# Attention units: projection products redealt over the units, a second output buffer, one group's evacuation and the output-projection groups placed earlier, row sums in another PSUM bank

## The chip, the cores and the metric

The kernel runs on one core of one Trainium2 chip. The metric is device time in microseconds (us), lower is better. Before the change the median of three runs was 2871.65 us (2866.72 to 2871.75). All times of the profile are from one further execution, taken with the hardware profiler; its own time is in the table below.

## The reference

Two trunk layers of a latent generator with a context prefix: layer 0 mixes tokens with differential attention, layer 1 with a state-space layer, and each is followed by an MLP. There are 1024 latent and 256 context tokens, 1024 channels, 8 heads with two 64-wide halves each. The change touches only the attention of layer 0:

```python
q_l = apply_rope(heads_qk(q_l), cos, sin) * scale
k_l = apply_rope(heads_qk(k_l), cos, sin)
...
def attend(q, k, v):
    s = jnp.einsum('bqhcd,bkhcd->bhcqk', q, k).astype(jnp.float32)
    p = jax.nn.softmax(s, axis=-1)
    w = p[:, :, 0] - lam * p[:, :, 1]
    o = jnp.einsum('bhqk,bkhe->bqhe', w.astype(v.dtype), v)
    return rmsnorm(o, subln_g) * (1.0 - lambda_init)
...
y_lat = jnp.einsum('bte,ed->btd', o_l, w_o)
```

Context queries see context keys only; latent queries see all 1280 keys. Everything is held to float32 accuracy: the kernel splits each operand into a high and a low half and makes three matmuls of each product (lines L132, L133 and L134 of the helper `mm3`: high by high, high by low, low by high).

## The kernel before

**Stages.** The attention stage runs from 219 to 895 us of the span. Ahead of it lie the norms, the value projection and head 0's queries and keys; behind it the rest of the output projection, the MLP of layer 0, and layer 1.

**Units.** The stage is a loop over 72 units, nine a head: n = 9h + u, with h from 0 to 7 and u from 0 to 8. Unit 0 of a head holds both tiles of 128 context queries; units 1 to 8 hold one tile of 128 latent queries each, against 1280 keys. Five more turns of the loop (n = 72 to 76) finish what is left. One turn does, for its own unit:

- scores on PE, 18 matmuls (L579) into PSUM banks 0 to 5 in three pieces of six; the third piece writes banks 2 and 3 beside their other contents
- two maxima on DVE (L592, 128x1280 each, which also copy the scores to SBUF), two exponentials on ACT (L602)
- on DVE the combination of the two softmaxes (`combine`, L610 to L613)

and for the unit before it:

- the transposes of the combined weights on PE (L625), in three parts: w0 (4 tiles), w1 (2) and w2 (4). w0 and w1 are as a rule split straight from PSUM, the high half by ACT (L631), the low half by DVE (L632); this is `direct`. w2 is copied out by ACT (L638) and split on POOL; this is `copied`.

Two units of queries make a pair. For a finished pair, PE multiplies the weights by the values into bank 6 (`values`), ACT copies the result to an output buffer (`pair_out`, L732), POOL squares it (L733) and a DMA stores it. A unit later PE sums the squares over each row (`pair_sums`, L739, 128x1 matmuls against ones) into bank 6, and ACT reads the sums (L740). In unit 5 of the next head, PE transposes the row factors (`norm_rows`, L758) into bank 6; five later turns multiply them in (`norm_pair`, L772 on DVE).

**Fills.** While DVE and ACT work on a unit, PE works on the projections of the next head. Those of queries and keys are six groups of eight products (three matmuls each), with 512 or 256 tokens a group, placed in units 0, 1, 2, 3, 5 and 7 (the table `AHEAD`). Each group accumulates in bank 7. `FILLS` says how its eight products are dealt over the three gaps of a unit: `(0, 1, 5, 8)` puts product 0 in the first gap, 1 to 4 in the second, 5 to 7 in the third; units not in the table have `(0, 0, 5, 8)`. Units 4, 6 and 8 have no group and another layout (`inside`). A 512-token group is emptied by `evac` (L528, L529), and then rotated, added and split by `sine`, `add` and `store` in the posts of later gaps (`next_post`; `store` is the split of ACT's L137 and DVE's L138). The two groups of context tokens (256 wide; keys in unit 1, queries in unit 2) have no rotation: their only step is `direct` (L523 on ACT, L524 on DVE). Unit 3's first product writes the bank that unit 2's group is emptied from.

**Head 7** has no next head to project. From n = 64 on it takes the output projection's groups for the first six heads instead (`wo_group`: six products of 512 columns, 18 matmuls, out by L855), one a turn, and head 7's own norm (`norm7`, L808 to L814; L812 is a 128x256 product into bank 6). Their weights are loaded and split in the same turns (`wsplit6`, its low half by POOL's L138, 128x1024).

**What sets the order.** The loop is under a manual schedule: PE, DVE, ACT and POOL execute in the order of the code. An instruction waits for the last conflicting access to the PSUM bank that it touches, even when it touches another part of the bank. In the stages behind, the framework's scheduler orders the engines by itself.

Of the kernel before, what the change touches and what calls it, by code (L numbers as in the profile page):

```python
# [13 lines left out]
KB = 256  # L14
# [56 lines left out]
class Prog:  # L71
# [578 lines left out]

    WO_BANKS = {8: 0, 9: 1, 0: 2, 1: 3, 2: 4, 3: 5, 4: 7}
    AHEAD = {0: (1, 0), 1: (1, 2), 2: (0, 2), 3: (1, 1), 5: (0, 0), 7: (0, 1)}
    FILLS = {0: (0, 1, 5, 8), 1: (0, 0, 0, 8), 2: (0, 2, 8, 8)}

    def b_start(self):

# [25 lines left out]
    def phase_b(self):  # L682
# [1 line left out]
        p0 = Ring([self.view(self.F1, 5 * i, (1280,)) for i in range(2)])  # L684
        p1 = self.view(self.F1, 10, (1280,))
        self.wraw = Ring([self.view(self.F1, 15 + 2 * i, (512,)) for i in range(3)])
        o = self.fv(6, 256)
        sq = self.adat
        self.raw = Ring([self.wv(0, 1024)])
        self.wr = Ring([(self.rv(4 * i, 4, 128), self.rv(4 * i + 2, 4, 128)) for i in range(4)])  # L690
# [37 lines left out]
        hst = self.fv(7, 3, 8, 10)  # L728

        def pair_out(h, pair):  # L730
            d = o7[pair % 2] if h == 7 else o
            nc.scalar.activation(d, pb[:, 0:256], AF.Copy)  # L732
            nc.gpsimd.tensor_tensor(sq, d, d, ALU.mult)  # L733
            if h < 7:
                self.dma(self.od[h, :, 256 * pair : 256 * pair + 256], d)

        def pair_sums(h, pair):
            for i in range(2):
                mm(pb[:, i : i + 1], sq[:, 128 * i : 128 * i + 128], self.ones, start=True, stop=True)  # L739
            nc.scalar.activation(hst[:, 1, h, 2 * pair : 2 * pair + 2], pb[:, 0:2], AF.Copy)  # L740


        def norm_calc(h, q0=0, q1=10):
# [11 lines left out]
        nloaded = []  # L755

        def norm_rows(h):
            nc.tensor.transpose(pb[0:10, 384:512], hst[:, 2, h], self.ident)  # L758
            rT = self.view(self.F1, 25, (128,))[0:10]
            nc.scalar.activation(rT, pb[0:10, 384:512], AF.Copy)  # L760
            self.dma(self.rsd[h], rT)

        def norm_load(h, pair):
# [93 lines left out]

            return [product(k) for k in range(6)], [out]

        wo_order = [8, 9] + list(range(8))  # L860

        self.qb = Ring([self.bank(7)])
        load_first()
# [12 lines left out]
        with self.manual():  # L876
            for n in range(72 + 5):
# [10 lines left out]
                if front:  # L888
# [10 lines left out]
                        qsplit = self.proj_weights(h + 2 if n else 1, 0)  # L899
                    if u == 5 and h < 6:  # L900
                        ksplit = self.proj_weights(h + 2, 1)
                if 64 <= n < 74:
                    groups = [wo_group(wo_order[n - 64])]
                fills = [[], [], []]
                if groups:
                    a = self.FILLS.get(u, (0, 0, 5, 8))
                    if n > 71:
                        a = (0, 2, 4, 6) if n == 72 else (0, 4, 6, 6)
                    fills = [groups[0][0][a[i] : a[i + 1]] for i in range(3)]
# [36 lines left out]
                if late or parts == 1:  # L946
                    if n == 73:
                        fill(0)
                    if inside:
                        values(*pv, 0, 5)  # L950
                        w0 = part(0, last)
                        values(*pv, 5)
                        w1, w2 = part(1, high), part(2, whole)
                    else:
                        if pv:
                            values(*pv)
                        w0, w1 = part(0, whole), part(1, high)
                    exps(0)
                    if inside:
                        direct(w0)  # L960
                    next_post()
                    exps(1)
                    if pv:
                        output(*pv)
                    split = norm()
                    if front:
                        self.combine(u, p, s0, sn)
                    if inside:
                        copied(w2, w1)
                    else:  # L970
                        direct(w0)
                        copied(w1)
                        if n != 73:
                            fill(0)
                        fill(1)
                        copied(part(2, whole))
                        fill(2)
                        do_sums()
                else:
                    if pv:  # L980
                        values(*pv)
                        output(*pv)
                    fill(0)
                    w0 = part(0, low)
                    if pv:
                        exps(0)
                    direct(w0)
                    next_post()
                    if not pv:
                        exps(0)  # L990
                    exps(1)
                    fill(1)
                    w2 = part(2, whole)
                    w1 = part(1, last[:, 256:512] if pv and h < 7 else self.bank(0)[:, 0:256] if n == 72 else high)
                    copied(w2)
                    if front:
                        self.combine(u, p, s0, sn)
                    direct(w1)
                    next_post()
                    fill(2)  # L1000
                    do_sums()
                    split = norm()
                if groups:
                    rest = groups[0][1]
                    rest[0]()
                    post += rest[1:]
                if split:
                    split()
# [1521 lines left out]
    def run(self):  # L2530
        tc = self.tc
        pool = lambda name, **kw: tc.tile_pool(name=name, bufs=1, **kw)
        with pool("cst") as self.cst, pool("psp", space=bass.MemoryType.PSUM) as psp, \
# [22 lines left out]
            with pool("r0") as rp, pool("fc") as cp:  # L2556
# [4 lines left out]
                    self.setup()  # L2561
                    self.phase_v()
                with pool("r1") as rp, pool("f1") as fp:
                    self.R1, self.F1 = rp.tile([128, 29 * KB], F32R, name="R1"), fp.tile([128, int(25.5 * KB)], F32, name="F1")
                    self.phase_b()
                for g in range(3):
                    for j in range(2):
# [72 lines left out]
```

## Time and profile before

| what | value |
|---|---|
| median of three runs | 2871.65 us (2866.72 to 2871.75) |
| the profiled execution, its own time | 2870.31 us |
| its span, first to last instruction | 2868.5 us |
| mean granted TensorE clock | 0.987 |
| attention stage, 219 to 895 us: busy PE / DVE / ACT / POOL | 621.1 / 525.3 / 381.2 / 370.0 of 676.0 us |
| everything behind 1000 us: busy PE / DVE | 1814.5 / 1336.8 of 1868.0 us |

How the rows are read. PE is the matmul engine, PEld its weight load, DVE the vector, ACT the scalar and POOL the GpSimd engine, SP the queue that issues DMAs. A row of windows gives a stretch of the span, its length, each engine's busy time with the number of instructions, the granted clock (1.00 is full speed), the DMA engines' mean share and GB/s. A row of waits gives the engine and line that waited, what it waited for, and total, count and longest. A row of the timeline gives start, duration, engine, line, operation, destination <- source, shape and number of instructions that run on; in brackets how long the engine was idle ahead of it, and what released it. L12 is line 12 of the kernel. PS is PSUM; H, R, F, W, FC, K, U are SBUF regions; od, Ad, Aa, wod are DRAM.

### The profile page before, as it was taken

How to read it: one execution, taken by the hardware profiler on the slowest of the kernel's cores; microseconds unless marked ns; L12 is line 12 of the kernel's file. 1: busy time of each engine (PE TensorE's matmuls, PEld its weight loads, DVE VectorE, ACT ScalarE, POOL GpSimd, SP SyncE). 2: the span in 40 equal slices, each digit the busy share in tenths (PEclk: the TensorE clock that was granted, in tenths of full speed). 3: DMA queues.
4: the chain of work that ended last, by engine and by line, in shares of the span. 5: the costliest groups of instructions: out<-in, count | busy, mean ns of one | idle time of the engine just before them, and what ended most of it. 6: DMA issues, size and time to landing. Idle time of an engine off the chain costs nothing. (4 is left out here: it accounts for less than half of the span.)

```text
span 2868.5 us, 43793 instructions
## 1 busy us (share of the span) xinstructions
PE 2721.0 (95%) x15645; PEld 2263.1 (79%) x15645; DVE 2026.8 (71%) x3024; ACT 1373.3 (48%) x2584; POOL 983.5 (34%) x822
## 2 busy tenths in 40 slices
PE   6999999999899899999999999899999999999999
PEld 4687878888677787878877778788887778888887
DVE  6357788888864477676698878799633597668566
ACT  3425555566553753333344445477443633344443
POOL 3314555565643700000020004588221243336314
PEclk9999999999999999999999999899999999999999
DMA  9953223333514448886699878479843144467544
GB/s 272 322 174 127 62 86 94 90 94 91 175 61 140 148 153 308 306 290 236 216 345 301 276 237 273 155 232 294 264 140 109 61 157 164 160 231 239 165 131 142
DMA packets 377447, 539.12 MB, mean 188 GB/s; under 512 B 38286, under 2 KB 231052, under 8 KB 374028
## 3 DMA queue, kind: packets, MB, share of 16 engines
q1 hardware_dynamic: 377228, 536.32, 57.5%
q8 instruction: 123, 2.02, 0.3%
q14 instruction: 96, 0.79, 0.1%
HBM read 367.54 MB, written 164.47 MB: 185 GB/s over the span
## 5 line engine op out<-in xcount | busy, mean ns | idle before, releaser
L132 PE MATMUL PS<-H 128*128 128x512 f32 x1072 | 420.5, 393 | 2.3 <-ACT H L137 1.5
L134 PE MATMUL PS<-H 128*128 128x512 f32 x1072 | 417.5, 390 | 3.0 <-DVE H L138 1.7
L133 PE MATMUL PS<-H 128*128 128x512 f32 x1072 | 417.7, 390 | 0.0
L132 PE MATMUL PS<-H,R 128*128 128x512 f32 (+1 forms) x828 | 307.9, 374 | 15.8 <-DVE R L524 11.6
L133 PE MATMUL PS<-H,R 128*128 128x512 f32 (+1 forms) x828 | 300.4, 363 | 0.0
L134 PE MATMUL PS<-H,R 128*128 128x512 f32 (+1 forms) x828 | 299.9, 363 | 0.0
L132 PEld LDWEIGHTS PS<-H 128*128 128x128 f32 x1072 | 201.1, 188 | 50.3 <-issue 6.2
L134 PEld LDWEIGHTS PS<-H 128*128 128x128 f32 x1072 | 201.2, 188 | 46.1 <-DVE H L138 2.6
L133 PEld LDWEIGHTS PS<-H 128*128 128x128 f32 x1072 | 201.3, 188 | 40.5
L132 PE MATMUL PS<-R,H 128*128 128x512 f32 x534 | 212.7, 399 | 3.9 <-ACT H L137 3.2
L137 ACT ACTIVATE R<-W 128x512 fp32r<-128x512 f32 (+1 forms) x185 | 129.7, 708 | 180.4 <-PE PS L133 107.6
L602 ACT ACTIVATE F<-F,stat 128x1280 f32<-128x1280 f32 x128 | 174.5, 1363 | 86.6 <-DVE F L592 86.3
L137 ACT ACTIVATE H<-U 128x640 fp32r<-128x640 f32 x216 | 131.9, 674 | 174.4 <-PE PS L133 147.3
L134 PE MATMUL PS<-R,H 128*128 128x512 f32 x534 | 210.7, 396 | 1.7 <-DVE H L138 1.7
L592 DVE TENSOR_SCALAR_CACHE_REDUCE F<-PS 128x1280 f32<-128x1280 f32 x128 | 185.4, 1485 | 34.8 <-PE PS L579 34.5
L133 PE MATMUL PS<-R,H 128*128 128x512 f32 x534 | 209.6, 393 | 0.0
L138 DVE TENSOR_TENSOR H<-U,H 128x640 fp32r<-128x640 f32 x216 | 165.6, 800 | 55.0 <-ACT H L137 54.9
L138 DVE TENSOR_TENSOR H<-W,H 128x512 fp32r<-128x512 f32 (+1 forms) x137 | 127.1, 939 | 103.2 <-ACT H L137 102.8
L132 PEld LDWEIGHTS PS<-H,R 128*128 128x128 f32 x828 | 158.6, 192 | 45.4 <-DVE R L524 13.3
L137 ACT ACTIVATE H<-W 128x512 fp32r<-128x512 f32 (+2 forms) x158 | 95.2, 613 | 189.8 <-PE PS L133 117.8
L134 PEld LDWEIGHTS PS<-H,R 128*128 128x128 f32 x828 | 158.5, 191 | 25.6 <-issue 0.8
L133 PEld LDWEIGHTS PS<-H,R 128*128 128x128 f32 x828 | 158.9, 192 | 21.1
(528 smaller groups left out, 6704.2 us busy)
## 6 DMA issues: line engine op xcount, KB each, us to landing
W<-in_mlp_w SPq DMA_DIRECT2D x176, 256.0 KB, 3.4
U<-Aa SPq DMA_DIRECT2D x108, 320.0 KB, 3.9
Aa<-FU SPq DMA_DIRECT2D x91, 320.0 KB, 4.5
Ad<-F SPq DMA_DIRECT2D x112, 256.0 KB, 2.7
W<-Ad SPq DMA_DIRECT2D x112, 256.0 KB, 2.7
FU<-in_mlp_w SPq DMA_DIRECT2D x32, 512.0 KB, 5.8
Ta<-FU SPq DMA_DIRECT2D x16, 1024.0 KB
U<-in_ada_w SPq DMA_DIRECT2D x32, 512.0 KB, 9.2
```

The source lines that it names most:

```text
L132: mm(out, ah, bh, start=first, stop=False, **kw)
L133: mm(out, ah, bl, start=False, stop=False, **kw)
L134: mm(out, al, bh, start=False, stop=last, **kw)
L137: self.nc.scalar.activation(hi, src, AF.Copy)
L138: (lo_eng or self.nc.vector).tensor_tensor(lo, src, hi.bitcast(F32), ALU.subtract)
L592: ts(p[c], self.PS[:, 1792 * c : 1792 * c + 1280], 1.0, None, ALU.mult, ALU.min, accum_out=sm[:, c : c + 1])
L602: nc.scalar.activation(p[c], p[c], AF.Exp, bias=sm[:, c : c + 1], scale=-1.0, accum_out=sn[:, 0:1] if c else s0[:, u + 1 : u + 2])
```

## The change

Six edits, all of them in the attention stage:

- `FILLS` and the default of a unit: in unit 0 products 0 to 2 stand in the first gap and 3 and 4 in the second (before: 0, and 1 to 4). In units 3, 5 and 7 product 0 moves from the second gap to the first. From n = 63 on, six-product groups are dealt 1, 3, 2 or, in turns of the other layout, 0, 4, 2 (before: 0, 5, 1 as a rule).
- `pair_out` takes one of two output buffers in turn for heads 0 to 6. The second lies at the end of `F1`, which is 1 KB larger.
- In unit 2 the context-token group is emptied right behind `direct(w1)`, ahead of `next_post` and `norm`. The call `fill(2)` stands ahead of `direct(w1)` in the code; on PE the order stays.
- `pair_sums` writes the last two columns of the first half of the score banks, `PS[:, 1790:1792]` in bank 3, except for head 7's pairs 3 and 4, which stay in bank 6.
- `norm_rows` transposes into `PS[0:10, 1280:1408]` in bank 2.
- The ten output-projection groups run in n = 63, 64, 65, 66, 68, 69, 70, 71, 72, 73 (before: 64 to 73).

```diff
-    FILLS = {0: (0, 1, 5, 8), 1: (0, 0, 0, 8), 2: (0, 2, 8, 8)}
+    FILLS = {0: (0, 3, 5, 8), 1: (0, 0, 0, 8), 2: (0, 2, 8, 8)}
...
-        o = self.fv(6, 256)
+        outs = Ring([self.fv(6, 256), self.view(self.F1, 25.5, (256,))])
...
-            d = o7[pair % 2] if h == 7 else o
+            d = o7[pair % 2] if h == 7 else outs.next()
...
         def pair_sums(h, pair):
+            b = pb[:, 0:2] if h == 7 and pair > 2 else self.PS[:, 1790:1792]
             for i in range(2):
-                mm(pb[:, i : i + 1], sq[:, 128 * i : 128 * i + 128], self.ones, start=True, stop=True)
-            nc.scalar.activation(hst[:, 1, h, 2 * pair : 2 * pair + 2], pb[:, 0:2], AF.Copy)
+                mm(b[:, i : i + 1], sq[:, 128 * i : 128 * i + 128], self.ones, start=True, stop=True)
+            nc.scalar.activation(hst[:, 1, h, 2 * pair : 2 * pair + 2], b, AF.Copy)
...
         def norm_rows(h):
-            nc.tensor.transpose(pb[0:10, 384:512], hst[:, 2, h], self.ident)
+            b = self.PS[0:10, 1280:1408]
+            nc.tensor.transpose(b, hst[:, 2, h], self.ident)
             rT = self.view(self.F1, 25, (128,))[0:10]
-            nc.scalar.activation(rT, pb[0:10, 384:512], AF.Copy)
+            nc.scalar.activation(rT, b, AF.Copy)
...
-        wo_order = [8, 9] + list(range(8))
+        wo_at = dict(zip((63, 64, 65, 66, 68, 69, 70, 71, 72, 73), [8, 9] + list(range(8))))
...
-                if 64 <= n < 74:
-                    groups = [wo_group(wo_order[n - 64])]
+                if n in wo_at:
+                    groups = [wo_group(wo_at[n])]
...
-                    a = self.FILLS.get(u, (0, 0, 5, 8))
+                    a = self.FILLS.get(u, (0, 1, 5, 8) if n < 63 else (0, 0, 4, 6) if late else (0, 1, 4, 6))
...
+                    fill(2)
                     direct(w1)
+                    now = groups and n < 63 and len(groups[0][1]) == 1
+                    if now:
+                        groups[0][1][0]()
                     next_post()
-                    fill(2)
                     do_sums()
                     split = norm()
                 if groups:
                     rest = groups[0][1]
-                    rest[0]()
+                    if late or parts == 1 or not now:
+                        rest[0]()
                     post += rest[1:]
...
-                    self.R1, self.F1 = rp.tile([128, 29 * KB], F32R, name="R1"), fp.tile([128, int(25.5 * KB)], F32, name="F1")
+                    self.R1, self.F1 = rp.tile([128, 29 * KB], F32R, name="R1"), fp.tile([128, int(26.5 * KB)], F32, name="F1")
```

The built programs show what moves. First DVE's queue in unit 2 of head 4 up to unit 3's first maxima, before. A row has line, operation, destination <- source, shape, and in brackets the engines or DMA queues that it waits for; L613 ends the combination, L632 is `direct(w1)`, L138 a store, L772 the norm of a pair, L524 the context group's evacuation, L592 the next unit's maxima:

```order
L613 SCALAR_TENSOR_TENSOR F_1851<-F_1851,stat 128x1280 [waits DVE_49]
L632 TENSOR_TENSOR R_110<-PS,R_110 128x2x128 [waits Activation_49]
L138 TENSOR_TENSOR R_1850<-FC,R_1850 128x512 [waits Activation_49]
L772 SCALAR_TENSOR_TENSOR W<-W,lamc 128x256 [waits DMAHW7_49,DMAHW0_49]
L524 SCALAR_TENSOR_TENSOR R_110<-PS,R_1850 128x256 [waits Activation_49]
L592 TENSOR_SCALAR F_1851,stat<-PS 128x1280 [waits PE_49]
```

The same piece of DVE's queue of the change (the lines behind `pair_sums` are one or two higher there):

```order
L613 SCALAR_TENSOR_TENSOR F_1851<-F_1851,stat 128x1280 [waits DVE_49]
L632 TENSOR_TENSOR R_110<-PS,R_110 128x2x128 [waits Activation_49]
L524 SCALAR_TENSOR_TENSOR R_110<-PS,R_1850 128x256 [waits Activation_49]
L138 TENSOR_TENSOR R_1850<-FC,R_1850 128x512 [waits Activation_49]
L774 SCALAR_TENSOR_TENSOR W<-W,lamc 128x256 [waits DMAHW7_49,DMAHW6_49]
L592 TENSOR_SCALAR F_1851,stat<-PS 128x1280 [waits PE_49]
```

L524 has passed the store and the norm of a pair.

Second, PE at the end of unit 1 and the start of unit 2 of a head, before: the last projection product, the row sums (L739) and the 18 score matmuls (L579; the last six are the third piece):

```order
L134 MATMUL PS<-H,R_110 128x256
L739 MATMUL PS<-lamc,adat 128x1 [waits Pool_49]
L739 MATMUL PS<-lamc,adat 128x1
L579 MATMUL PS<-R_1850 128x512 x12
L579 MATMUL PS<-R_1850 128x256 [waits DVE_49]
L579 MATMUL PS<-R_1850 128x256 x5
```

And PE at the same place in the change, where the sums are L740:

```order
L134 MATMUL PS<-H,R_110 128x256
L740 MATMUL PS<-lamc,adat 128x1 [waits DVE_49,Pool_49]
L740 MATMUL PS<-lamc,adat 128x1
L579 MATMUL PS<-R_1850 128x512 x12
L579 MATMUL PS<-R_1850 128x256
L579 MATMUL PS<-R_1850 128x256 [waits Activation_49]
L579 MATMUL PS<-R_1850 128x256 x4
```

The order of the instructions is the same; the sums wait for DVE as well (in this unit L632 of w0, which reads bank 3), and the third piece of the scores waits for ACT (the reading of the sums). In the other units the sums waited for DVE and POOL before, and wait for ACT (the copy of w2) and POOL now.

Third, PE in unit 63 (n = 63, head 7's unit 0). Before, the end of its scores (L579), ten transposes and the sums stood there, with unit 64's scores behind:

```order
L579 MATMUL PS<-R_1850 128x256 x4
L579 MATMUL PS<-R_1850,R_110 128x256 x2
L625 MATMUL PS<-ident,F_1851 128x128 x10
L739 MATMUL PS<-lamc,adat 128x1 x2
L579 MATMUL PS<-R_1850 128x512 x12
```

In the change the products of the first output-projection group (L132 to L134, 128x512) stand between and behind the transposes; the piece has the first products in the middle gap and those after the other transposes:

```order
L625 MATMUL PS<-ident,F_1851 128x128 x3
L132 MATMUL PS<-R_110,H 128x512 [waits DMAHW6_49]
L133 MATMUL PS<-R_110,H 128x512
L134 MATMUL PS<-R_110,H 128x512 [waits DMAHW7_49]
L132 MATMUL PS<-R_1850,H 128x512 [waits DMAHW0_49,Activation_49]
L133 MATMUL PS<-R_1850,H 128x512 [waits Pool_49]
L134 MATMUL PS<-R_1850,H 128x512 [waits DMAHW1_49]
L625 MATMUL PS<-ident,F_1851 128x128 x4
L625 MATMUL PS<-ident,F_1851 128x128 [waits DVE_49]
L625 MATMUL PS<-ident,F_1851 128x128
L132 MATMUL PS<-R_1850,H 128x512 [waits DMAHW0_49]
```

The second product of this piece waits for ACT and POOL, the two engines that split the group's weights; the transposes of the unit stand behind it.

## Prediction

> **What bounds the kernel now.** I read the page first, then the windows, then the waits of the attention stage, then the timeline of single units.
>
> ```profile
> span 2868.5 us, 43793 instructions
> PE 2721.0 (95%) x15645; PEld 2263.1 (79%) x15645; DVE 2026.8 (71%) x3024; ACT 1373.3 (48%) x2584; POOL 983.5 (34%) x822
> 541.00:621.00 80.00, 75.26 (x536) 64.95 (x534) 66.56 (x107) 47.43 (x95) 46.31 (x42) 0.98 0.28 85
> 780.00:895.00 115.00, 104.30 (x626) 87.30 (x627) 64.05 (x108) 48.92 (x94) 50.94 (x59) 0.94 0.23 76
> 895.00:1000.00 105.00, 93.17 (x445) 74.13 (x444) 48.72 (x54) 60.34 (x120) 58.73 (x69) 0.98 0.49 157
> 1000.00:1100.00 100.00, 100.00 (x543) 84.83 (x543) 75.44 (x116) 54.79 (x110) 5.08 (x2) 1.00 0.56 186
> ```
>
> PE is the bound: 95% of the span, and 100 of 100 us once the attention stage and the stage behind it are over (last row). So a microsecond that PE stops waiting in attention (219 to 895 us) is a microsecond of the kernel, as long as PE doesn't wait for it later. One head is the window 541 to 621: PE is idle 4.7 of 80 us, DVE busy 66.6. The idle has few names:
>
> ```profile
> PE PS L625 <- DVE F L613: 16.3, 21, 2.3
> PE PS L132 <- DVE R L524: 11.6, 7, 2.1
> PE PS L739 <- POOL R L641: 8.4, 14, 1.7
> PE PS L758 <- ACT FC L740: 2.1, 6, 0.4
> ACT FC L732 <- DMA od<-FC: 7.2, 3, 2.9
> ```
>
> Each row is total, count, longest. The transposes (L625) wait for the weights that DVE makes (L613); the first product of unit 3 (L132) waits for the direct group's evacuation (L524); the row sums (L739) and the row transpose (L758) wait for a bank. I go through these unit by unit.
>
> **Unit 3: the direct group emptied sooner, one product ahead.** Head 4, PE and then DVE:
>
> ```profile
> 558.11 2.01 PE L579 MATMUL PS<-R 64*128 64x512 f32 x18
> 560.23 0.66 PE L625 MATMUL PS<-ident,F 128*128 128x128 f32 x4
> 562.98 0.80 PE L132 MATMUL PS<-H,R 128*128 128x512 f32 x1 [2.10 <-DVE R L524]
> 566.65 0.40 PE L132 MATMUL PS<-H,R 128*128 128x512 f32 x1
> 568.03 0.82 PE L625 MATMUL PS<-ident,F 128*128 128x128 f32 x6
> 571.19 2.00 PE L579 MATMUL PS<-R 64*128 64x512 f32 x18
> 560.09 0.42 DVE L632 TENSOR_TENSOR R<-PS,R 128x256 fp32r<-128x256 f32 x1
> 560.42 0.76 DVE L138 TENSOR_TENSOR R<-FC,R 128x512 fp32r<-128x512 f32 x1
> 561.11 1.48 DVE L772 SCALAR_TENSOR_TENSOR W<-W,lamc 128x256 f32<-128x256 f32 x1
> 562.51 0.41 DVE L524 SCALAR_TENSOR_TENSOR R<-PS,R 128x256 fp32r<-128x256 f32 x1
> 565.67 0.68 DVE L632 TENSOR_TENSOR R<-PS,R 128x512 fp32r<-128x512 f32 x1
> ```
>
> From 566.65 to 568.03 PE does two products, six matmuls: 0.23 us each, 0.69 a product. The five products from 562.98 to 568.03 took 5.05 instead of 3.45: 1.6 lost at half clock. L524 stands behind L138 and L772; in the change it follows L632 at once and ends at 560.42 + 0.42 = 560.9. PE ends its scores at 560.1, so it waits 0.8 for the first product, then transposes and does four products (2.8): 564.9. The next transposes for the bank of the first (two of the six) need the L632 that ends at 566.35: DVE's own queue, which the change doesn't shorten. Then three products and the sums (0.2 + 2.1 + 0.45): the next scores at 569.2 instead of 571.2. So of 2.1 us of wait and 1.6 of half clock this head gets 2.0; without half clock the same steps give about 1.0, since L632 bounds them. Of the seven waits of the row three (heads 2 to 4) were followed by half clock: 3 x 2.0 + 4 x 1.0 = **-10.0**. What ACT and DVE had queued behind the old L524 (the store's L138, then the maxima) moves by L524's 0.4 at most.
>
> ```profile
> 480.00:490.00 10.00, 8.03 (x39) 6.30 (x36) 8.62 (x14) 5.03 (x9) 3.52 (x4) 0.83 0.14 42
> 640.00:650.00 10.00, 7.58 (x40) 5.94 (x39) 8.06 (x12) 5.12 (x11) 5.04 (x5) 1.00 0.12 40
> ```
>
> The granted clock was 0.83 in the ten microseconds of one such wait and 1.00 in another of the same length: a wait of 2 us sometimes costs a stretch of half clock (0.17 x 10 us lost is 3.4 us at half speed). The Trainium skill, "TensorE: Matmul & The Clock Gate" (Part 1), says that the clock halves after a whole idle window of about 3.4 us, the window running freely. By that rule a wait of 2 us would not do it, the dips would stay with a shorter one, and the forecast would be 2844.7 instead of the 2842.4 below. The trace decides for neither: the first row has a dip at 2 us of idle, the second has none. So I count only half of what I credit to dips, here 3 x 1.0 and in head 7 1.5: **+2.3** on the sum (0 to +4.5).
>
> **Two output buffers.** ACT's L732 waited for the store of the one buffer (last row of the waits, three times, 2.9 the longest), and in heads 2 and 3 PE waited for L732:
>
> ```profile
> 394.19 0.66 PE L625 MATMUL PS<-ident,F 128*128 128x128 f32 x4 [0.75 <-ACT FC L732]
> 475.06 0.66 PE L625 MATMUL PS<-ident,F 128*128 128x128 f32 x4 [1.06 <-ACT FC L732]
> ```
>
> Two outputs follow each other only in units 1 and 2; with a second buffer the next store to be waited for is two units old: 0.75 + 1.06 = **-1.8** (at the least 0, if DVE sets unit 3 in these heads too). SP issues as many stores of the same size as before.
>
> **Units 5, 7 and 0: products redealt.** One product more stands ahead of the transposes in 5 and 7, two more in 0.
>
> ```profile
> 590.36 1.49 DVE L592 TENSOR_SCALAR_CACHE_REDUCE F<-PS 128x1280 f32<-128x1280 f32 x1 [1.07 <-PE PS L579]
> 580.50 0.63 PE L625 MATMUL PS<-ident,F 128*128 128x128 f32 x4 [0.50 <-DVE F L613]
> 535.48 0.63 PE L625 MATMUL PS<-ident,F 128*128 128x128 f32 x4 [1.37 <-DVE F L613]
> 620.62 1.43 DVE L138 TENSOR_TENSOR R<-FC,R 128x512 fp32r<-128x512 f32 x1
> 623.38 1.49 DVE L592 TENSOR_SCALAR_CACHE_REDUCE F<-PS 128x1280 f32<-128x1280 f32 x1 [0.34 <-PE PS L579]
> 550.63 0.68 DVE L632 TENSOR_TENSOR R<-PS,R 128x512 fp32r<-128x512 f32 x1
> 550.85 0.50 PE L739 MATMUL PS<-lamc,adat 128*128 128x1 f32 x4
> ```
>
> Unit 5: 0.69 covers the 0.50, and L758, in another bank, no longer waits its 0.35; DVE is free from 589.3 and idle before unit 6's maxima (590.36, for the scores), so it is kept: 6 x 0.85 + 0.5 in head 0 = **-5.6**. In units 7, 8 and 0 the waits vanish too (0.5 + 0.3 + 1.4), but what is late next is DVE: before unit 1's maxima (623.38) it idled 0.34 us only. Its L138 took 1.43 against 0.76 in unit 3, beside a POOL instruction that starts when PE's last transposes are copied, now 1.4 us sooner: perhaps 0.6 more. So unit 1 comes 0.95 sooner. And unit 1 has a new wait: its sums now lie in the bank that L632 reads, until 551.3, where PE began them at 550.85: 0.5 lost. Behind them on PE stand unit 2's scores, and DVE waits for these. Net 0.4 a head, six heads: **-2.4** (between +3, the new wait alone, and the full 2.2 a head, -13).
>
> **Sums in free half banks.** Elsewhere they wait for ACT's copy alone instead of L632; that is the 8.4 us of L739, in units 3 and 7 counted above, in head 7 below. The next scores' third piece is now behind ACT's read of the sums; it has 1.3 us (12 of 18 matmuls of a 2.0 us block), and ACT was waiting for PE each time:
>
> ```profile
> 587.80 0.17 ACT L740 ACTIVATE FC<-PS 128x2 f32<-128x2 f32 x1 [1.28 <-PE PS L739]
> ```
>
> **Head 7: wo groups a unit sooner.**
>
> ```profile
> 772.50 1.06 PE L625 MATMUL PS<-ident,F 128*128 128x128 f32 x8 [2.27 <-DVE F L613]
> 782.25 0.98 PE L739 MATMUL PS<-lamc,adat 128*128 128x1 f32 x4 [6.14 <-DVE R L632]
> 783.16 3.57 PE L579 MATMUL PS<-R 64*128 64x512 f32 x18
> 777.04 2.34 POOL L138 TENSOR_TENSOR R<-W,R 128x1024 fp32r<-128x1024 f32 x1
> 813.04 0.58 PE L739 MATMUL PS<-lamc,adat 128*128 128x1 f32 x4 [1.56 <-POOL R L641]
> 833.59 0.58 PE L739 MATMUL PS<-lamc,adat 128*128 128x1 f32 x4 [1.67 <-POOL R L641]
> ```
>
> Unit 63 holds over 8 us of idle. A wo group (18 matmuls, 4.1 us) goes in. It doesn't run through: its fifth product needs the weights whose low half POOL finishes at 779.4, so PE still stands some 5 us, and then has 0.7, the transposes, 0.7 and the sums left: unit 64 at about 782.2, **-1.0**. Behind the waiting product stand unit 63's last transposes; POOL and ACT get them late, but what they make of them is read only 4 us into unit 64. The gain comes later: unit 67 has no group, **-4.1**. Unit 66's sums lose their 1.56 (**-1.7** with the moved products). In 68 and 70 the wait passes from L739 to the norm's product (L812), which writes the bank that L632 still reads: of 1.67 each I keep 1.0, **-2.1** with L758. Half-clock after unit 63 and in 68 to 71, shorter: **-1.5**.
>
> **The sum.** -10.0 - 1.8 - 5.6 - 2.4 - 1.0 - 4.1 - 1.7 - 2.1 - 1.5 + 2.3 = -27.9. The profiled execution took 2870.31 us (1.8 around its span) and the median of the three runs is 2871.65; against the profiled one that is 2842.4, and I say **2843**. The stage behind attention is reordered by the framework's scheduler at no cost that I can read; it idles 11.8 of 105 us now, and I allow 4 us each way.
>
> **The rivals.**
>
> DVE and POOL take the gain. DVE is busy 66.6 of 80 us in a head of which PE would need only 76; L138 and L772 last 1.4 to 1.5 us where they meet a POOL instruction, about 0.5 to 0.8 where not. Two more such meetings a head, 0.8 each, over seven heads is 11 us, and units 5 and 0 give back the rest: a gain of 12, 2858. The row that speaks against it is the idle of DVE before unit 1 and before unit 6. The Trainium skill, "SBUF — State Buffer", holds that the port pair that DVE and GpSimd share is locked by whichever starts first, for the whole instruction. The 1.43 and 1.48 agree with a lock of that kind. Chance 0.18.
>
> The stage behind attention is ordered worse: its 11.8 us of idle grow by as much: gain 16, 2854. Chance 0.08.
>
> The move of the wo groups is worth nothing since unit 67, now without a group, waits for the wT of 66: gain 28 - 4 - 1 = 23, 2847; inside the forecast's range. Chance 0.08.
>
> Slower: the sums' bank. If ACT reads the sums behind an exponential (the maxima of a unit release 1.4 us instructions) instead of at once, the next scores stop in their third piece. It decides from a read that ends over 1.3 us after the sums. Five sums a head, 35 in seven heads, one exponential late is about 1.0 each: +35 against -28, 2877. Against it: ACT was idle 1.28 us before the read in the row above. Chance 0.04. That the order isn't changed as said is out: the built programs show it.
>
> **Chances.** Forecast 0.62 (2834 to 2850), the rivals as given. Below 0.2%, 5.7 us, a measurement of this kernel can hardly tell a change from none. Faster by more 0.88 (forecast, both middle rivals, most of DVE's), within 0.07, slower 0.05. The range that leaves out 2 in 10: 2833 (no dip left, 4 us from the stage behind, 3 more from units 7 to 1) to 2860 (DVE's rival and 2 us of the last stage).
>
> **What would show it.** L132's wait for L524 at about 0.8 in place of 2.1, and a new one of about 1 us for L632 at unit 3's second transposes. L625's waits for L613 in units 5 and 7 gone, in 0 near nothing. A new wait of the sums for L632 in unit 1, 0.5 us or more. In unit 63 a matmul that waits 5 us for POOL's L138. Unit 67 4 us shorter. No wait of ACT's pair output for a store. It is wrong if the head window (80 us) shrinks by less than 2 us, or if the stage behind attention takes over 109 us.

## The result, and the profile after

The changed kernel took 2847.1 us, median of four runs (2843.75 to 2852.37), against 2869.18 (four runs) before: a ratio of 0.9926, 95% interval 0.9904 to 0.9949. The profiled execution took 2845.55 us. First the page of the change, its head and the busy times:

```profile
span 2843.8 us, 43784 instructions
PE 2713.8 (95%) x15645; PEld 2259.5 (79%) x15645; DVE 2025.9 (71%) x3024; ACT 1368.1 (48%) x2584; POOL 978.9 (34%) x822
```

The span is 24.7 us shorter with the same matmuls. Next its windows: one head (unit 1 of head 4 to unit 1 of head 5), and the stage behind attention:

```profile
532.30:609.20 76.90, 73.48 (x533) 63.54 (x535) 65.65 (x107) 46.80 (x96) 45.74 (x42) 1.00 0.30 89
895.00:1000.00 105.00, 96.61 (x512) 80.08 (x511) 60.85 (x74) 73.76 (x151) 62.61 (x70) 1.00 0.42 140
```

From unit 1 to unit 1 this head now takes 76.9 us, at full clock, and DVE is busy 65.7 of them. The same stretch before took 79.5, where the prediction's window of 80 us is a little wider:

```profile
541.90:621.40 79.50, 74.76 (x534) 64.54 (x533) 66.06 (x107) 47.43 (x95) 45.81 (x42) 0.98 0.29 86
```

So the head is 2.6 us shorter, and DVE's work in it is the same. Then PE's waits in the attention stage, as total, count, longest:

```profile
PE PS L132 <- DVE R L524: 9.0, 7, 1.4
PE PS L740 <- DVE R L632: 7.3, 6, 1.2
PE PS L625 <- DVE F L613: 4.2, 7, 0.7
...
PE PS L133 <- POOL R L138: 2.8, 1, 2.8
```

The transposes' wait for L613 fell from 16.3 to 4.2, the first product's for L524 from 11.6 to 9.0. New is the second row: the row sums (now L740) wait for L632, six times, once a head. In unit 1 to 2 of head 4 that is

```profile
542.85 0.58 PE L740 MATMUL PS<-lamc,adat 128*128 128x1 f32 x4 [1.24 <-DVE R L632]
```

How long each unit takes is the distance from one block of scores (L579) to the next on PE's timeline. The last unit, n = 71, has no block behind it and is left out. Summed over heads 0 to 6, in us:

| unit | before | change | difference |
|---|---|---|---|
| 0 | 63.8 | 59.9 | -3.9 |
| 1 | 66.2 | 76.3 | +10.1 |
| 2 | 50.1 | 49.3 | -0.9 |
| 3 | 84.5 | 76.8 | -7.8 |
| 5 | 71.6 | 64.7 | -6.9 |
| 7 | 70.7 | 64.4 | -6.3 |
| 4, 6, 8 | 143.1 | 143.7 | +0.6 |
| head 7, n = 63 to 70 | 89.8 | 82.0 | -7.8 |
| all 71 | 639.9 | 617.0 | -22.8 |

The rest, about 2 us, lies behind: from unit 71's scores to the end it is 2009.4 us before and 2007.3 after. Part of the gain is clock. In these units the profile before has nine times 3.41 us of half clock, that of the change five times; at 1.7 us lost in each that is 6.8 of the 22.8 us, an estimate which takes PE's time as counting in full. The row that stands out is unit 1: 9.4 us a head before, 11.2 after.

### The profile page after: what moved, and what is told of

It is laid out like the page before. It is cut to its first block, busy times and chain, and to the rows that moved or that the text cites. A ratio compares the mean times of both kernels' runs of the same rounds, so it can differ in the third digit from the quotient of the medians.

```text
span 2843.8 us, 43784 instructions
## 1 busy us (share of the span) xinstructions
PE 2713.8 (95%) x15645; PEld 2259.5 (79%) x15645; DVE 2025.9 (71%) x3024; ACT 1368.1 (48%) x2584; POOL 978.9 (34%) x822
## 5 line engine op out<-in xcount | busy, mean ns | idle before, releaser
L132 PE MATMUL PS<-H 128*128 128x512 f32 x1072 | 421.0, 394 | 2.5 <-ACT H L137 1.8
L134 PE MATMUL PS<-H 128*128 128x512 f32 x1072 | 418.0, 391 | 2.9 <-DVE H L138 1.6
L132 PE MATMUL PS<-H,R 128*128 128x512 f32 (+1 forms) x828 | 308.2, 374 | 12.5 <-DVE R L524 9.0
L134 PE MATMUL PS<-H,R 128*128 128x512 f32 (+1 forms) x828 | 298.3, 361 | 0.0
L132 PEld LDWEIGHTS PS<-H 128*128 128x128 f32 x1072 | 201.3, 188 | 50.3 <-issue 6.2
L134 PEld LDWEIGHTS PS<-H 128*128 128x128 f32 x1072 | 201.3, 188 | 46.0 <-DVE H L138 2.4
L132 PE MATMUL PS<-R,H 128*128 128x512 f32 x534 | 213.7, 401 | 5.3 <-ACT H L137 3.3
L134 PE MATMUL PS<-R,H 128*128 128x512 f32 x534 | 211.4, 397 | 1.8 <-DVE H L138 1.8
L592 DVE TENSOR_SCALAR_CACHE_REDUCE F<-PS 128x1280 f32<-128x1280 f32 x128 | 185.2, 1483 | 22.5 <-PE PS L579 22.5
L138 DVE TENSOR_TENSOR H<-U,H 128x640 fp32r<-128x640 f32 x216 | 162.2, 785 | 50.9 <-ACT H L137 50.6
L138 DVE TENSOR_TENSOR H<-W,H 128x512 fp32r<-128x512 f32 (+1 forms) x137 | 124.5, 919 | 102.0 <-ACT H L137 101.5
L132 PEld LDWEIGHTS PS<-H,R 128*128 128x128 f32 x828 | 157.6, 191 | 42.5 <-DVE R L524 10.4
L134 PEld LDWEIGHTS PS<-H,R 128*128 128x128 f32 x828 | 157.4, 190 | 25.1 <-issue 0.8
```

The costliest lines, as they stand in the source:

```text
L132: mm(out, ah, bh, start=first, stop=False, **kw)
L134: mm(out, al, bh, start=False, stop=last, **kw)
L138: (lo_eng or self.nc.vector).tensor_tensor(lo, src, hi.bitcast(F32), ALU.subtract)
L592: ts(p[c], self.PS[:, 1792 * c : 1792 * c + 1280], 1.0, None, ALU.mult, ALU.min, accum_out=sm[:, c : c + 1])
```

## The experiments

All are compared with the same kernel before, the change with 2847.1. The first eight edit the change; b1 and b2 edit the kernel before; c1 and c2 look for more. "71 units" is the sum of the units as in the table above, from one profile each. e7 was run twice, the others four times or more.

| run | edit | median us | ratio to before, 95% | 71 units |
|---|---|---|---|---|
| before | | 2869 | | 639.9 |
| change | | 2847.1 | 0.9904 to 0.9949 | 617.0 |
| e1 | unit 1's sums in bank 6 | 2833.2 | 0.9859 to 0.9896 | 607.4 |
| e2 | unit 0 dealt as before | 2852.1 | 0.9924 to 0.9954 | 624.0 |
| e3 | wo groups from n = 64 | 2848.6 | 0.9911 to 0.9941 | 618.8 |
| e4 | context group emptied late | 2858.7 | 0.9945 to 0.9972 | 628.8 |
| e5 | one output buffer | 2847.0 | 0.9904 to 0.9934 | 620.8 |
| e6 | all sums in bank 6 | 2881.5 | 1.0029 to 1.0064 | 655.0 |
| e7 | no L642 in unit 0 | 2838.3 | 0.9870 to 0.9909 | 609.7 |
| e8 | e1, and n = 63 dealt later | 2838.9 | 0.9870 to 0.9903 | 607.5 |
| b1 | before, sums in bank 3 only | 2857.1 | 0.9948 to 0.9975 | 627.7 |
| b2 | before, products redealt only | 2896.6 | 1.0079 to 1.0124 | 670.1 |
| c1 | e1, w1 ahead of the combination | 2838.8 | 0.9881 to 0.9925 | 612.0 |
| c2 | c1, two products ahead in unit 3 | 2842.1 | 0.9889 to 0.9922 | 612.2 |

### Unit 1: the bank (e1)

```diff
-            b = pb[:, 0:2] if h == 7 and pair > 2 else self.PS[:, 1790:1792]
+            b = pb[:, 0:2] if pair == 4 or h == 7 and pair > 2 else self.PS[:, 1790:1792]
```

> The change, with the row sums of unit 1 (pair 4) in bank 6 again. In the change unit 1 of heads 1 to 6 takes 10.75 to 11.20 us against 9.39 before; 1.24 of it is PE's sums waiting for DVE's L632. Theory (the bank): that wait goes, unit 1 takes 9.95, six heads give -7.4 us: about 2840 against 2847. Rival (DVE's queue is late and is the bound whatever the sums do): PE then waits as long for DVE in unit 2, units 1 and 2 together stay at 18.0, and the time at 2847.

Unit 1 fell from 11.19 to 9.71 in heads 2 to 6, and from 76.3 to 68.9 over seven: -7.4 (heads 1 to 6 gave 8.7, head 0 lost 1.3 to half clock), and unit 2 did not grow (6.80). The bank's theory held. The median fell by 13.9, the profiled execution by 10.4; of that, 2.2 is unit 64, which ran at half clock in the profile of the change (12.8) and not here (10.6). The other 4 us of the median have no cause shown. 2833.2 us is the lowest median of the study, though the intervals of e7, e8, c1 and c2 overlap this one.

### Unit 1: why DVE is late there (e2, e7)

In the change DVE starts unit 1's maxima 3.19 us after the scores' start (535.36 against 532.17); in the kernel before it was 2.03 to 2.05 in heads 1 to 6, when the scores were done. What DVE did ahead of that in the change, in unit 0 of head 4, with POOL beside it:

```profile
530.44 0.93 DVE L613 SCALAR_TENSOR_TENSOR F<-F,stat 128x256 f32<-128x256 f32 x1
...
531.89 1.61 DVE L613 SCALAR_TENSOR_TENSOR F<-F,stat 128x256 f32<-128x256 f32 x1
...
535.36 1.47 DVE L592 TENSOR_SCALAR_CACHE_REDUCE F<-PS 128x1280 f32<-128x1280 f32 x1
530.35 0.74 POOL L138 TENSOR_TENSOR F<-F 128x256 fp32r<-128x256 f32 x1
531.06 0.79 POOL L641 TENSOR_SCALAR R<-F 128x512 fp32r<-128x512 f32 x1
531.93 1.28 POOL L642 TENSOR_TENSOR R<-F,R 128x512 fp32r<-128x512 f32 x1
```

In head 4 the two L613 took 0.49 each before the change. Now the second lies over POOL's L642 and ends 0.3 behind it. The meeting itself is not new, though. In the kernel before, the same L642 lay beside DVE's L138, which took 1.79 (0.68 in the change):

```profile
540.84 1.79 DVE L138 TENSOR_TENSOR R<-FC,R 128x512 fp32r<-128x512 f32 x1
540.81 1.28 POOL L642 TENSOR_TENSOR R<-F,R 128x512 fp32r<-128x512 f32 x1
```

From unit 0's last maximum to unit 1's first, DVE took 7.2 to 7.3 us in heads 1 to 6 before, with 0.3 to 0.5 of it idle. In heads 2 to 6 of the change it takes 6.98, with nothing idle. DVE's work in unit 0 is as long as it was; PE is sooner, and DVE has no time to spare.

```diff
-    def w_copy(self, tb, hi, lo):
+    def w_copy(self, tb, hi, lo, low=True):
...
-            self.nc.gpsimd.tensor_tensor(lo, t, hi.bitcast(F32), ALU.subtract)
+            if low:
+                self.nc.gpsimd.tensor_tensor(lo, t, hi.bitcast(F32), ALU.subtract)
...
-                    for f in [self.w_copy(*w) for w in ws if w]:
+                    for f in [self.w_copy(*w, u > 0) for w in ws if w]:
```

> The change without POOL's L642 (the low half of w2) in unit 0's turn of every head; the weights' low half of these tiles is not computed. Theory (two of DVE's L613, 128x256, last 0.93 and 1.61 us in the change's unit 0 beside a POOL instruction, against 0.48 without one, and this makes DVE late for unit 1): the second L613 takes 0.48, DVE starts unit 1's maxima 1.1 us sooner (2.05 to 2.1 after the scores' start, not 3.19), the sums' wait for L632 falls from 1.24 to about 0.5, unit 1 takes about 10.0 instead of 11.19: -7 us, about 2840. Rival (DVE's lateness comes from PE's earlier scores alone, not from POOL): L613 stays long or unit 1 stays at 11.1: 2847.

The same place in this run, DVE and then PE (whose sums are L741 here):

```profile
522.74 0.93 DVE L613 SCALAR_TENSOR_TENSOR F<-F,stat 128x256 f32<-128x256 f32 x1
...
524.19 0.49 DVE L613 SCALAR_TENSOR_TENSOR F<-F,stat 128x256 f32<-128x256 f32 x1
...
526.52 1.48 DVE L592 TENSOR_SCALAR_CACHE_REDUCE F<-PS 128x1280 f32<-128x1280 f32 x1
534.03 0.58 PE L741 MATMUL PS<-lamc,adat 128*128 128x1 f32 x4 [0.45 <-DVE R L632]
```

The second L613 is back at 0.49, the sums wait 0.45, unit 1 takes 10.07: the theory held in every number. Without the meeting 1.1 of unit 1's 1.8 us go, and 0.7 is left, the bank's (10.07 against 9.39 before). This split depends on what is undone first: e1 leaves the meeting and takes out 1.5. And it prices the meeting, which the kernel before had too; it does not make it the reason why unit 1 became longer.

```diff
-    FILLS = {0: (0, 3, 5, 8), 1: (0, 0, 0, 8), 2: (0, 2, 8, 8)}
+    FILLS = {0: (0, 1, 5, 8), 1: (0, 0, 0, 8), 2: (0, 2, 8, 8)}
```

> The change, with unit 0's products dealt (0, 1, 5, 8) as before. Theory (the two products ahead of the transposes bring PE's work of unit 1 on while DVE's queue keeps its length, so that DVE is late there): unit 0 goes back from 8.88 to 9.65, unit 1 falls from 11.19 to about 9.9 (9.39 and 0.5 for the sums' bank), six heads give -3.1 us: about 2844. Rival (unit 1 is late for another reason, and the products in unit 0 are a gain of their own): unit 0 +0.77, unit 1 unchanged, +4.6 us: about 2852.

Neither came out whole. Unit 1 fell as the theory has it, to 10.06 in heads 1, 2, 5 and 6, with the sums' wait at 0.46 (10.2 and 11.15 in heads 4 and 3), and DVE starts its maxima 2.04 after the scores again: with the products as before, PE is no longer early. But unit 0 went to 10.3 to 11.8, not 9.65. PE's wait ahead of unit 0's transposes, and the windows of unit 0 in heads 4 and 5:

```profile
528.44 1.09 PE L625 MATMUL PS<-ident,F 128*128 128x128 f32 x4 [1.97 <-DVE F L613]
524.62:536.32 11.70, 9.73 (x53) 7.95 (x52) 9.32 (x23) 6.66 (x19) 7.40 (x8) 0.85 0.39 109
603.27:613.54 10.27, 8.29 (x53) 6.72 (x52) 9.42 (x23) 6.67 (x19) 7.60 (x8) 1.00 0.40 125
```

The wait is 1.97 against 1.37 before: DVE comes 0.6 late out of unit 8 (its L613 starts 1.87 after unit 0's scores, 1.22 before), since unit 7 got shorter for PE and not for DVE. Four of the six waits were followed by half clock. The redealt products of unit 0 cover this; they are worth 7.0 us in the units, while the medians, 2852.1 and 2847.1, have intervals that overlap.

### The sums' place and the redealt products (e6, b1, b2)

```diff
-            b = pb[:, 0:2] if h == 7 and pair > 2 else self.PS[:, 1790:1792]
+            b = pb[:, 0:2]
```

> The change with all row sums in bank 6, as before (the row transpose stays in bank 2). Theory (the new place frees units 3, 7, 66, 68 and 70 of the wait for L632 and gives unit 1 one): unit 1 -1.24 a head, -7.4 in all; units 3 and 7 +0.3 a head, +4; unit 66 +1.6; 68 and 70 +1.3 together; the sum is near nothing, 2846. Rival (in units 3 and 7 the sums now come after L632 anyway, since one product more stands ahead of the transposes): only head 7's units grow, +3, against -7.4: about 2843.

Both expectations failed, by 35 us and more: the kernel became slower than before. PE's waits in the attention stage:

```profile
PE PS L740 <- DVE R L632: 26.5, 13, 2.4
PE PS L740 <- POOL R L641: 14.9, 17, 2.6
```

The second row is the same wait as the first: each of its 17 sums starts 0.15 us after an L632 ends, as the 13 do. Unit 1 did fall by 10.2 over the seven heads, but unit 7 grew by 16.0, 0 by 8.4, 3 by 7.9, 5 by 7.6 and 8 by 6.9. That asks for the two edits alone, on the kernel before: b1 has the new `pair_sums` and nothing else; b2 has

```diff
-    FILLS = {0: (0, 1, 5, 8), 1: (0, 0, 0, 8), 2: (0, 2, 8, 8)}
+    FILLS = {0: (0, 3, 5, 8), 1: (0, 0, 0, 8), 2: (0, 2, 8, 8)}
...
-                    a = self.FILLS.get(u, (0, 0, 5, 8))
+                    a = self.FILLS.get(u, (0, 1, 5, 8) if n < 63 else (0, 0, 5, 8)) if n < 63 or u > 2 else {0: (0, 1, 5, 8), 1: (0, 0, 0, 8), 2: (0, 2, 8, 8)}[u]
```

> The kernel before with one edit: the row sums in bank 3, as in the change (unit 1 too). Theory (the edits need each other: the sums' place alone frees only the short waits of before): units 3 and 7 -0.3 a head, unit 5 -0.35, unit 63 -3.6, unit 66 -1.6, units 68 and 70 -1.3, unit 1 +0.5: -10 us, about 2859. Rival (the place of the sums is worth by itself what undoing it in the change cost, 34 us): about 2835.

> The kernel before with one edit: the products of units 0, 3, 5 and 7 dealt as in the change, for the heads' own projections (n < 63). Theory (the sums in bank 6 stand behind w1's L632, whose weights come no sooner; a product that is moved ahead only makes this wait longer, and longer waits bring half clock): about 2869 + 34 - 10 = 2893 by the undone sums less what the other edits gave, slower than before in any case. Rival (additive edits, the forecast's sum): unit 5 -0.5, unit 0 -0.8, unit 7 -0.5 a head: -11 us, about 2858.

They came out at 2857.1 and 2896.6, close to what the theory of edits that need each other gave (2859 and 2893). By medians: the sums alone -11, the products alone +28, the whole change -22. Why, is read from unit 7 of head 4 in b2, PE and DVE:

```profile
621.23 0.75 PE L739 MATMUL PS<-lamc,adat 128*128 128x1 f32 x4 [2.31 <-DVE R L632]
618.08 2.67 DVE L613 SCALAR_TENSOR_TENSOR F<-F,stat 128x1280 f32<-128x1280 f32 x1
620.67 0.41 DVE L632 TENSOR_TENSOR R<-PS,R 128x256 fp32r<-128x256 f32 x1
```

and in the change, PE, DVE and ACT:

```profile
592.89 0.50 PE L740 MATMUL PS<-lamc,adat 128*128 128x1 f32 x4
592.21 2.67 DVE L613 SCALAR_TENSOR_TENSOR F<-F,stat 128x1280 f32<-128x1280 f32 x1
590.88 0.59 ACT L638 ACTIVATE F<-PS 128x512 f32<-128x512 f32 x1
```

In both, PE finishes its products before DVE's long L613 ends. In bank 6 the sums then wait until w1's L632, behind L613, is done. In bank 3 they need only ACT's copy (L638), done at 591.5, and PE goes on to the next scores while L613 still runs. Half clock adds to it: the units of b2 hold 17 times 3.41 us of it against nine before, some 14 of the 30 us that they grew (an estimate, at half speed).

### Head 7 (e3, e8)

```diff
-        wo_at = dict(zip((63, 64, 65, 66, 68, 69, 70, 71, 72, 73), [8, 9] + list(range(8))))
+        wo_at = dict(zip((64, 65, 66, 67, 68, 69, 70, 71, 72, 73), [8, 9] + list(range(8))))
```

> The change, with the ten output-projection groups in n = 64 to 73 as before. Theory of the forecast (the move is worth unit 67's 4.1 us and 1.0 in unit 63): +5 us, about 2852. Rival (the sums' bank alone ends unit 63's wait, whose 6.14 us were the sums behind L632, and the group that was put there takes the place of it): unit 63 falls from 14.0 to about 8.8, unit 64 grows by 0.9 since DVE is late, unit 67 grows by 4.2: no change, about 2847.

The rival held: 2848.6, which cannot be told from 2847.1. Unit 63 took 10.3 (14.0 in the change), 64 12.6, 67 12.6 (6.8), 68 9.9 (11.1): head 7 together 82.7 against 82.0. In b1, with the sums moved and the groups not, it is 82.3, and unit 63's sums wait thus:

```profile
775.08 0.99 PE L740 MATMUL PS<-lamc,adat 128*128 128x1 f32 x4 [1.12 <-ACT F L638]
```

The 6.14 us of before became 1.12, for ACT's copy. Nearly all of head 7's 7.8 us is the sums' place. With the group in unit 63, PE and POOL of the change show the wait for L138 that was forecast as 5 us, at 2.84, and one for ACT's half of the same weights ahead of it:

```profile
760.80 0.50 PE L132 MATMUL PS<-R,H 128*128 128x512 f32 x1 [1.24 <-ACT R L137]
764.14 0.80 PE L133 MATMUL PS<-R,H 128*128 128x512 f32 x1 [2.84 <-POOL R L138]
761.74 2.35 POOL L138 TENSOR_TENSOR R<-W,R 128x1024 fp32r<-128x1024 f32 x1
```

In the change this group is dealt 3, 2, 1: n = 63 is a unit 0, and units 0 to 2 go by `FILLS` in head 7 too, not by the 1, 3, 2 that the list of edits gives from n = 63 on.

```diff
-                    a = self.FILLS.get(u, (0, 1, 5, 8) if n < 63 else (0, 0, 4, 6) if late else (0, 1, 4, 6))
+                    a = (0, 3, 4, 6) if n == 63 else self.FILLS.get(u, (0, 1, 5, 8) if n < 63 else (0, 0, 4, 6) if late else (0, 1, 4, 6))
```

> The change with unit 1's sums in bank 6 (2833 in the earlier run) and in n = 63 the six products dealt (0, 3, 4, 6): the product that waits for the weights of POOL's L138 stands behind the unit's last transposes instead of ahead of them. Theory (unit 63's 13.9 us are a chain: product waits for POOL, transposes behind it, then POOL and ACT again): POOL's L138 ends 9.5 us into the unit, two products and the sums behind it: 11.2, -2.7 us, about 2830. Rival (the transposes' followers on POOL and DVE are not what unit 64 waits for): unit 63 shorter by 0.7 at most, unit 64 the same: about 2833.

Unit 63 fell by 1.2 against e1 (13.87 to 12.69), half of what was expected, and unit 64 ran at half clock (13.0 against 10.6). 2838.9 can't be told from e1's 2833.2, since the intervals overlap; the run shows no gain.

### The context group and the output buffer (e4, e5)

```diff
-                    now = groups and n < 63 and len(groups[0][1]) == 1
+                    now = False
```

> The change, with unit 2's context group emptied behind the store and the norm of a pair, as before; unit 3 keeps the one product ahead of its transposes. Theory (L524's place in DVE's queue sets unit 3): L132's wait goes from 1.3 back to 2.1 and some of the seven heads fall to half clock behind it: +1.0 to +1.6 a head, +7 to +11 us, about 2854 to 2858. Rival (unit 3's gain came from the product put ahead of the transposes, which the late evacuation only delays): under 0.3 a head, about 2848.

+11.6 by medians, 11.7 in the 71 units, of which unit 3 is 6.8; L132's waits went from 9.0 to

```profile
PE PS L132 <- DVE R L524: 16.1, 7, 2.9
```

The theory held. With one product ahead of the transposes the old place costs more wait than it did before the change (11.6).

```diff
-        outs = Ring([self.fv(6, 256), self.view(self.F1, 25.5, (256,))])
+        outs = Ring([self.fv(6, 256)])
```

> The change with one output buffer for heads 0 to 6, as before. Theory of the forecast (ACT's pair output waits for the last store, and PE's transposes of unit 2 wait for it in two heads): unit 2 of some heads grows by 0.75 to 1.06, ACT's L732 waits for a DMA again; +1.8 us, about 2849. Rival (DVE sets unit 3 in these heads, so that a transpose that comes later costs nothing): the wait comes back, the sum of units 2 and 3 does not grow, 2847.

By its time the rival held: 2847.0. ACT's wait for a store came back only once, where it was three times and 7.2 us in all before:

```profile
ACT FC L732 <- DMA od<-FC: 2.1, 1, 2.1
```

and PE waited 0.26 for it, in one head. So the rival's reason, that DVE sets unit 3, was hardly put to the test here. Unit 2 grew by 4.9 over the seven heads, mostly by half clock behind the sums' wait of unit 1 (granted clock 0.80 in three heads, one in the change; no wait in the unit itself), and unit 3 shrank by 2.0. By time the run cannot tell 1.8 us from nothing.

### More to be had in unit 3? (c1, c2)

```diff
+                    now = groups and n < 63 and len(groups[0][1]) == 1
+                    if now:
+                        direct(w1)
+                        groups[0][1][0]()
                     if front:
                         self.combine(u, p, s0, sn)
                     fill(2)
-                    direct(w1)
-                    now = groups and n < 63 and len(groups[0][1]) == 1
-                    if now:
-                        groups[0][1][0]()
+                    if not now:
+                        direct(w1)
```

(on e1; c2 also deals unit 3's products `(0, 2, 5, 8)`)

> The change with unit 1's sums in bank 6 and, in unit 2, direct(w1) and the context group's evacuation ahead of the combination on DVE instead of behind it. In the change L524 ends 3.3 us into unit 3, since L523 waits on ACT for w1's L632, which stands behind L613 (1.55). Theory: L132's wait of 1.33 falls under 0.3, what is late next is w0's transposes for the combination, 0.4 to 0.8 later than now; unit 3 -0.5 to -1.0, seven heads -3 to -7: about 2828 beside 2833. Rival (DVE's queue from L613 to the maxima sets unit 3, in either order): unit 3 the same within 0.2, 2833.

> As the run with w1 ahead of the combination, with two products of unit 3 instead of one ahead of its transposes. Theory: the second product covers the later combination: unit 3 another 0.3 to 0.7 a head shorter than with one, 2824 to 2827. Rival (DVE's queue sets unit 3): the same as with one product.

Neither theory came true: 2838.8 and 2842.1, no better than 2833.2, and unit 3 took 0.33 a head longer in both, a little more than the rival's 0.2. In unit 3 of head 4, PE and then DVE, in c1:

```profile
550.10 0.50 PE L132 MATMUL PS<-H,R 128*128 128x512 f32 x1 [0.20 <-DVE R L524]
552.18 0.66 PE L625 MATMUL PS<-ident,F 128*128 128x128 f32 x4 [1.11 <-DVE F L613]
550.57 1.55 DVE L613 SCALAR_TENSOR_TENSOR F<-F,stat 128x1280 f32<-128x1280 f32 x1
...
553.03 1.49 DVE L592 TENSOR_SCALAR_CACHE_REDUCE F<-PS 128x1280 f32<-128x1280 f32 x1
```

The wait of 1.32 became 0.20, and 1.11 stands at the next instruction instead. The maxima start 5.1 us into the unit (4.8 in e1), and unit 3 takes 11.49 against 11.15. The unit grew by what the maxima are later: DVE sets it, in either order.

## Why the prediction was right, and where it wasn't

The time, 2847.1, lies in the range and 4 us above the forecast; the spans of the profiles differ by 24.7 where the sum said 27.9. Where PE waits and which waits end was mostly right; that the sum came out is in part luck, as the fifth point below shows. The terms:

- **Unit 3: -10.0 forecast, -7.8 measured.** The mechanism was right (e4 gives it back). The step that was mis-sized is "Of the seven waits of the row three ... 4 x 1.0": the seven were counted as alike, but heads 0 and 1 had waited 0.69 and gained 0.05 and 0.02. The three with half clock gained 1.8 to 2.1, the other two 0.9 and 1.0. Half clock did not return in unit 3 of the change, so its share of the +2.3 was not needed. L524 ends 3.3 us into the unit, not 2.8, since L523 waits on ACT for w1's L632; so the first wait is 1.32 and not 0.8, and the wait for L632 at the second transposes, "about 1 us", is 0.17.
- **Output buffers: -1.8 forecast, nothing that e5 can tell.** The lower end, which the prediction kept, fits. With the other edits in, PE's two waits of 0.75 and 1.06 shrink to one of 0.26 even with one buffer.
- **Unit 5: -5.6 forecast, -6.9 measured.** The wait for L613 is gone, as argued. But the product that covers it gives nothing alone (+0.4 in b2), while the sums' place alone gives 3.8 (b1).
- **Units 7, 8, 0 and 1: -2.4 forecast, +0.5 measured** (-6.3, +0.6, -3.9, +10.1). That DVE is late next, and that the sums in unit 1 wait for L632, was right. Two terms were mis-sized. "So unit 1 comes 0.95 sooner": from unit 7's scores to unit 1's first maximum the six heads take 2.9 less in all, 0.5 each. The 0.6 in it was a meeting of L138 with POOL that would end; it did (1.79 to 0.68), but L613 met the same instruction instead (0.49 to 1.61). "0.5 lost": from its first maximum to the next scores unit 1 takes 8.00 instead of 7.34, 0.66 lost. PE's own wait, 1.24, is longer, since PE comes early. The wait for L613 in unit 0, "near nothing" in the forecast, is 0.6 a head. The contention rival asked for two more meetings a head; DVE's busy time in the head went from 66.1 to 65.7, so they did not come.
- **Sums in free half banks: the step that failed.** "That is the 8.4 us of L739, in units 3 and 7 counted above" prices the new place by the waits that it ends. Undone, it costs 34 us: the gains of units 3, 5, 7 and 0, put down to the products, are there only while the sums don't stand behind L632 (e6 loses them all, b2 never has them). The sum came out since both edits are in the change, and nothing in the working asked for that. For the products alone the same working would have said some 11 us faster, and 28 slower was measured.
- **Head 7: -10.4 forecast (with its half clock), -7.8 measured.** Unit 67 lost 4.2 and unit 66 1.7, as said; unit 63 gained nothing, 68 and 70 1.3 of 2.1. But the cause given for the 4.1 was wrong: e3 and b1 have the gain without the move, in unit 63. The fifth product's wait for POOL was 2.84, not 5, but a wait of 1.24 for ACT stood ahead of it, and half clock behind. The rival "worth nothing" was right in its result, wrong in its reason (unit 67 does not wait for unit 66's weights).
- **The slower rival**, an exponential ahead of ACT's reading of the sums, did not come: the third piece of the scores waited for ACT 0.7 us in all, for copies, not for the sums.
- **The stage behind** took 2 us less, within the 4 allowed. From unit 71's scores to the end the profiles of all runs lie between 2004.8 and 2013.7, so 2 us says nothing of the edits.

## What to carry to other kernels

Before pricing work that is moved ahead on the bound engine, list what stands behind it there and what each of those waits for: the next wait may take all of it (+28 us here) until a second edit removes it, and then neither has a price of its own. A meeting of a second engine with a third (L138 or L613 with L642) cost nothing while the second had time to spare; once the bound engine came sooner, it cost 1.1 us a head. Where a second engine is busy 66 of 77 us, follow its queue from unit to unit; a wait of the first engine that vanishes (1.32 to 0.20) proves nothing until the next unit starts earlier.

## What the runs showed of the hardware

**Half clock after short waits.** In e2 PE waited 1.96 to 2.06 us in the same place in heads 1 to 6; unit 0 then took 10.3 in two heads and 11.7 to 11.8 in four, and the granted clock, in one of either, was 1.00 and 0.85. The clock rows tell why. In every profile here half clock comes in stretches of 3.41 us or a multiple of it (up to 13.65; only the one that the end of the kernel cuts differs), and within a run all of them start on one grid of 3.41 us. Heads 4 and 5 of e2, the grid's window with the wait and the one behind it:

```profile
524.83:528.24 3.41, 1.64 (x15) 1.03 (x13) 3.08 (x6) 2.49 (x6) 1.91 (x2) 1.00 0.85 231
528.25:531.66 3.41, 3.22 (x10) 2.77 (x11) 2.83 (x11) 2.04 (x8) 3.24 (x5) 0.50 0.16 55
603.34:606.75 3.41, 1.78 (x15) 1.17 (x15) 3.08 (x5) 2.65 (x6) 1.75 (x2) 1.00 0.67 205
606.76:610.17 3.41, 3.06 (x16) 2.61 (x17) 3.07 (x13) 2.34 (x8) 3.24 (x4) 1.00 0.27 89
```

In the four heads with half clock PE was busy 0.42 to 0.48 of the window that held the wait, in the two others 0.52 and 0.57. In e4 a wait of 2.87 that two windows share (busy 0.64 and 0.52) was not followed by half clock (unit 3: 12.04), one of 2.86 inside one window (0.16) was (13.62). The two rows that the prediction sets beside each other differ in the same way: at 480 us one window holds the whole wait (0.42), at 640 two share it (0.71 and 0.68). Busy time is not the whole rule: behind the sums' wait of 1.24 in unit 1 the window is busy 0.63 to 0.64, and half clock followed in one of four such heads of the change and in three of four of e5. The Trainium skill, "TensorE: Matmul & The Clock Gate" (Part 1), has the clock halve after an idle window of about 3.4 us that runs freely. The window's length and its running freely agree with these traces; that a whole window must be idle does not, since a window with PE busy for 1.64 of its 3.41 us sufficed.

**DVE beside POOL.** L613, 128x256, lasts 0.48 to 0.49 alone and up to 1.61 where POOL's L642 lies beside it; without that instruction it was 0.49 again. L138, 128x512, lasts 0.68 alone and 1.79 beside the same L642. The Trainium skill, "SBUF — State Buffer", holds that the port pair that the two share is locked for a whole instruction. The lengths agree with that. Which of the two came first they don't settle: in the profile L613 starts 0.04 ahead of L642 and still ends 0.3 behind it.
